# A two-layer decoder trunk in fp32 pairs: forget gates beside a values projection, shifted weight tiles, a second bank for retention, and another border between the layers

## Chip, cores and metric

The kernel runs on one core of a Trainium2 chip. The metric is the device time of one execution in microseconds; before the change the median of three runs was 1018.92 (1017.69 to 1019.12).

## What is computed

One sequence of 512 tokens of width 1024 passes two layers, each with a normalization ahead and a residual sum behind, and a last normalization. The core of the reference:

```python
def even_layer(x, g_norm, w_in, b_f, w_out):
    z = rms_norm(x, g_norm) @ w_in
    qa, ka, va, ga, fa, qb, kb, vb, gb = jnp.split(z, cuts, axis=-1)
    log_f = jax.nn.log_sigmoid(fa.astype(f32) + b_f.astype(f32))
    ya = forgetting_attention(hA(qa), hA(ka), hA(va), log_f).reshape(Bsz, S, WIDTH_FOX)
    yb = dilated_attention(hB(qb), hB(kb), hB(vb)).reshape(Bsz, S, WIDTH_DIL)
    y = jnp.concatenate([ya * jax.nn.silu(ga), yb * jax.nn.silu(gb)], axis=-1)
    return x + y @ w_out

def odd_layer(x, g_norm, w_in, w_out):
    z = rms_norm(x, g_norm) @ w_in
    q, k, v, g = jnp.split(z, [qk_w, 2 * qk_w, 2 * qk_w + v_w], axis=-1)
    q = rotate(q.reshape(Bsz, S, N_HEADS_RET, RET_QK_DIM))
    k = rotate(k.reshape(Bsz, S, N_HEADS_RET, RET_QK_DIM)) * (RET_QK_DIM ** -0.5)
    y = retention(q, k, v.reshape(Bsz, S, N_HEADS_RET, RET_V_DIM))
    y = head_group_norm(y).reshape(Bsz, S, v_w).astype(x.dtype)
    return x + (y * jax.nn.silu(g)) @ w_out
```

Layer 0 has 16 forgetting heads (causal softmax attention whose logits get differences of the running sum c of log_f, one gate for each of the 16 heads and each token) and 16 dilated heads, all 64 wide. Layer 1 has 4 retention heads with q and k 256 wide and v and gate 512 wide: o at token t is the sum over s up to t of a decay times (q_t . k_s) v_s, then a normalization over the head.

## The kernel before, in words

Tokens are held as 4 tiles of 128. `xres` is the residual stream (token on the partition), and `xT` is the normalized input, transposed (feature on the partition). Every factor of a wide matmul is kept as two fp32r numbers, a high part and the rest, and a product is three matmuls, hi·hi, hi·lo and lo·hi, by `three` (L199, L200, L201). `split` makes the pair: ScalarE copies the high part (L140), VectorE subtracts it (L142).

*Weights* come in chunks of 512 KB in the order of a list, `plan`. `load_next` issues the DMA of the next one from SP into one of three buffers `w_raw`; `split_next` splits the oldest into `w_h` and `w_l`, 1,024 floats per partition each, in two operations of 512 on each engine; `weights` hands out the oldest split chunk.

*Layer 0* has 8 head groups of 4 heads in the order D F F F F D D D (D dilated, F forgetting). A group's projections are its values by `proj_tokens` (result `pt`, token on the partition: the stationary operand is a block of xT, the moving one 256 columns of the weights; two chunks, 96 matmuls), its keys and queries by `proj_features` (result `pf`: weights stationary, 512 columns of xT moving; 48 × 2 matmuls), and its gates, again by `proj_features`. The attention of a head goes in steps of one query block: logits into `ps_s`, VectorE adds the bias and takes the smallest, ScalarE takes the exponential, POOL divides (`softmax_block`); a head later its blocks are transposed into `ps_pt` and split (`transpose_block`), then multiplied with the values into `ps_o` (`pv_block`); `finish_head` forms y, POOL multiplies it by the gate, and a split makes `yh` and `yl`. `interleave` spreads fillers over the steps of a group by their estimated time: the group's gate projection, the next group's values, an output projection where `OUTS` has one (result `po`, added to xres at L296), and the next group's keys and queries. In the last group, 7, the filler beside its gates is the output projection of groups 5 and 6.

*Forget gates* (`forget_gates`) run as the first filler of group 0: 16 matmuls with the 16 gate columns of the weights into `pfa` (L381, L382), the bias by ScalarE, four transposes into `ps_zt` (L387), the log sigmoid in some fifteen small operations on VectorE and ScalarE (tile `fg`), transposes into `ps_lt` (L425), a running sum by VectorE's scan (L430), transposes into `ps_ct` (L433), and a DMA to `c_dram`. `fox_bias` loads a head's row from there into all partitions (`cs`) and lets POOL make the bias of a block.

*The border*: after group 7 its output projection runs by token tile (`last_out`, two chunks, 12 matmuls per tile). After a tile's half, `last_tile` takes its sum of squares (L127) and POOL multiplies the half by the gain of layer 1 (L584); after both halves come the reciprocal root (`rstd_of`, L105 to L111), the scaling by ScalarE (L588), transposes into `ps_xt` (L151), and the split into xT.

*Layer 1*: head 0's projections come before any head's steps: values (`proj_tokens` twice), gate g by `proj_wide` (result `pw`, 512 columns of weights moving), keys and queries. `rotate_done` rotates k and q, with POOL and a split at the end. Then per head `scores` (`ps_a`), `retain` (the sums into the bank `ps_r`; statistics, `yn` at L773 by VectorE, the gate on POOL at L774), and `y_block` (transposes into `ps_yt`, L782), spread over fillers, which are the next head's projections and the previous one's output projection. Accumulators of TensorE: three banks for projections (pool `pp`), two for logits and scores (`ps_s`), two for transposes (`ps_t`) and one (`ps_o`) for a head's output and `ps_r`.

The order on POOL is as the program is written; on the other engines a scheduler of the framework sets it.

## Time and profile before

| | |
|---|---|
| three runs | 1019.12, 1017.69, 1018.92 us, median 1018.92 |
| the profiled execution | 1019.2 us, of which the span of the trace is 1017.2 |
| mean granted clock of TensorE | 0.996 of full |
| TensorE (PE) busy | 992.6 us, 98% of the span, 5,170 matmuls |
| weight loads (PEld) | 840.3 us, beside the matmuls |
| VectorE (DVE), ScalarE (ACT), POOL busy | 637.0, 481.6, 240.0 us |
| DMA | 100.5 MB, mean 99 GB/s |

A row of a timeline gives the start and the length of one instruction in microseconds, its engine, line, operation, "written tile<-tiles read", the stationary operand's shape (of a matmul) and the written one's, and in brackets how long the engine was idle before it and what released it. Matmuls overlap: one starts before the last has ended, so what each costs is the spacing from start to start. A row of the waits gives the waiting engine, tile and line, what it waited for, and the total in microseconds, the count and the longest one. A group's row gives the count, the busy time, the mean length in ns, and the idle time ahead with its releasers.

### The profile page before, as it was taken

Reading aid. Unit: us, or ns where it says so; the run is one execution under the profiler, and the core shown is the slowest. Engines: PE = TensorE matmul, PEld = TensorE weight load, DVE = VectorE, ACT = ScalarE, POOL = GpSimd, SP = SyncE. Lnnn points to the kernel's source line nnn. Section 1 sums busy time; section 2 is a strip of 40 time slices with the busy share of each in tenths; the row PEclk is TensorE's granted clock in tenths of the full one; section 3 lists DMA queues with packets and bytes.
Section 4 is the critical chain, followed back from the end, with each engine's and each line's share of the span. In section 5 each row is a group of like instructions: output and inputs, shape, how many; then the busy total and the mean of one; then the engine's idle time right before and its main releaser. Section 6 shows DMA issues by size and latency. Waiting matters only on the chain.

```text
span 1017.2 us, 14317 instructions
## 1 busy us (share of the span) xinstructions
PE 992.6 (98%) x5170; PEld 840.3 (83%) x5170; DVE 637.0 (63%) x1382; ACT 481.6 (47%) x987; POOL 240.0 (24%) x340
## 2 busy tenths in 40 slices
PE   8999999999999999999999989999999999999997
PEld 7878898898888988988988779877888888888875
DVE  6465676576576676665667773477545844683476
ACT  6355565555545645554657573333323332333233
POOL 1011444444344442211212130013100300030012
PEclk9999999999999999999999999999999999999999
DMA  7554677544557884337333125222222231322112
GB/s 205 115 127 87 137 91 98 146 100 93 140 101 111 120 91 128 81 66 136 72 110 99 58 65 189 83 84 83 83 63 84 84 102 62 104 84 83 63 42 83
DMA packets 73288, 100.50 MB, mean 99 GB/s; under 512 B 5233, under 2 KB 48497, under 8 KB 73090
## 3 DMA queue, kind: packets, MB, share of 16 engines
q1 hardware_dynamic: 73218, 99.60, 42.4%
q8 instruction: 40, 0.66, 0.3%
q14 instruction: 30, 0.25, 0.1%
HBM read 84.87 MB, written 2.13 MB: 86 GB/s over the span
## 4 chain that ended last, share of the span: by engine, by line
PE 86%; DVE 7%; ACT 2%; DMA 2%; issue 2%; POOL 1%; DVEq 0%; POOLq 0%; ACTq 0%; SPq 0%
PE pf L199 10%; PE pf L200 10%; PE pf L201 10%; PE pw L200 5%; PE pw L201 5%; PE pw L199 5%; PE po L199 5%; PE po L201 5%; PE po L200 5%; PE pt L201 3%; PE pt L199 3%; PE pt L200 3%; PE ps_pt L502 3%; PE ps_o L515 2%; PE ps_o L514 2%; PE ps_s L488 2%
## 5 line engine op out<-in xcount | busy, mean ns | idle before, releaser
L142 DVE TENSOR_TENSOR w_l<-w_raw,w_h 128x512 fp32r<-128x512 f32 x288 | 210.7, 758 | 97.7 <-ACT w_h L140 83.9
L140 ACT ACTIVATE w_h<-w_raw 128x512 fp32r<-128x512 f32 x288 | 169.8, 628 | 187.3 <-PE pf L200 56.3
L199 PE MATMUL pf<-xT,w_h 128*128 128x512 f32 x512 | 201.5, 394 | 0.0
L201 PE MATMUL pf<-xT,w_l 128*128 128x512 f32 x512 | 200.5, 392 | 0.0
L200 PE MATMUL pf<-xT,w_h 128*128 128x512 f32 x512 | 200.3, 391 | 0.0
L495 POOL TENSOR_SCALAR pi<-pi,st 128x512 f32<-128x512 f32 (+3 forms) x128 | 74.5, 583 | 363.4 <-DVE st L494 333.4
L201 PEld LDWEIGHTS pf<-xT,w_l 128*128 128x128 f32 x512 | 96.1, 188 | 21.1
L199 PEld LDWEIGHTS pf<-xT,w_h 128*128 128x128 f32 x512 | 96.2, 188 | 18.3
L200 PEld LDWEIGHTS pf<-xT,w_h 128*128 128x128 f32 x512 | 96.2, 188 | 18.1
L140 ACT ACTIVATE pth<-ps_pt 128x512 fp32r<-128x512 f32 (+3 forms) x128 | 55.2, 431 | 97.0 <-PE ps_pt L502 85.6
L201 PE MATMUL pt<-w_h,xT 128*128 128x256 f32 x320 | 90.8, 284 | 1.6 <-DVE xT L142 1.6
L199 PE MATMUL pt<-w_h,xT 128*128 128x256 f32 x320 | 91.4, 286 | 0.1
L200 PE MATMUL pt<-w_l,xT 128*128 128x256 f32 x320 | 90.8, 284 | 0.0
L199 PE MATMUL pw<-w_h,xT 128*128 128x512 f32 x224 | 88.4, 395 | 0.0
L200 PE MATMUL pw<-w_l,xT 128*128 128x512 f32 x224 | 87.9, 393 | 0.0
L201 PE MATMUL pw<-w_h,xT 128*128 128x512 f32 x224 | 87.9, 392 | 0.0
L493 ACT ACTIVATE pi<-pi,st 128x512 f32<-128x512 f32 (+3 forms) x128 | 71.5, 559 | 33.4 <-DVE st L491 32.7
L774 POOL TENSOR_TENSOR yn<-yn,gate 128x512 f32<-128x512 f32 x16 | 21.0, 1313 | 265.0 <-DVE yn L773 255.5
L296 DVE TENSOR_TENSOR xres<-po,xres 128x512 f32<-128x512 f32 x88 | 59.6, 684 | 26.4 <-PE po L201 26.0
L142 DVE TENSOR_TENSOR ptl<-ps_pt,pth 128x512 fp32r<-128x512 f32 (+3 forms) x128 | 62.3, 488 | 20.4 <-ACT pth L140 18.6
L201 PEld LDWEIGHTS pt<-w_h,xT 128*128 128x128 f32 x320 | 61.2, 191 | 1.8 <-DVE xT L142 1.8
L199 PEld LDWEIGHTS pt<-w_h,xT 128*128 128x128 f32 x320 | 61.1, 191 | 1.1 <-ACT xT L140 0.6
(178 smaller groups left out, 1898.0 us busy)
## 6 DMA issues: line engine op xcount, KB each, us to landing
w_raw<-in_even_w_in_dram SPq DMA_DIRECT2D x64, 512.0 KB, 5.4
w_raw<-in_odd_w_in_dram SPq DMA_DIRECT2D x48, 512.0 KB, 3.6
w_raw<-in_even_w_out_dram SPq DMA_DIRECT2D x16, 512.0 KB, 4.1
w_raw<-in_odd_w_out_dram SPq DMA_DIRECT2D x16, 512.0 KB, 3.5
qb<-qa SPq DMA_DIRECT2D x32, 128.0 KB, 2.8
qb<-qa SPq DMA_DIRECT2D x16, 256.0 KB, 3.2
qa<-qa SPq DMA_DIRECT2D x32, 128.0 KB, 3.0
cs<-c_dram SPq DMA_DIRECT2D x16, 256.0 KB, 3.6
```

What stands on the lines that cost most here:

```text
L140: act.activation(hi, src, AF.Copy, scale=scale)
L142: dve.tensor_tensor(lo, src, r32(hi), ALU.subtract)
L199: pe.matmul(ps, lhsT=ah, rhs=bh, start=first, stop=False)
L200: pe.matmul(ps, lhsT=ah, rhs=bl, start=False, stop=False)
L201: pe.matmul(ps, lhsT=al, rhs=bh, start=False, stop=last)
L296: dve.tensor_tensor(xr, ps, xr, ALU.add)
L488: pe.matmul(ps[:, 0:n], lhsT=q[:, 1, qs], rhs=k[:, 0:n], start=False, stop=True)
L493: act.activation(pi[:, 0:n], pi[:, 0:n], AF.Exp, bias=st[:, 0:1], scale=-1.0, accum_out=st[:, 1:2])
L495: pool.tensor_scalar(pi[:, 0:n], pi[:, 0:n], st[:, 2:3], 1.0, ALU.mult, ALU.mult)
L502: pe.transpose(pt[:, (i - j) * P:(i - j + 1) * P], hs["p"][i][:, j * P:(j + 1) * P], ident)
L514: pe.matmul(po[:, j * P:S], lhsT=v, rhs=th[:, 0:n], start=(j == 0), stop=False)
L774: pool.tensor_tensor(yn, yn, r["g"][:, i, :], ALU.mult)
```

## The change

1. The 16 gate columns ride in the values projection of the first forgetting group (`proj_more`, 96 matmuls with 272 columns in place of 256, result `pm`). The 16 matmuls into `pfa` and the transposes into `ps_zt` go. The gate chain is cut in three: `forget_gates` behind that projection, `forget_sums` at step 14 of the 16 of the next keys projection, `forget_turn` at step 5 of the queries. The gate weights and the bias come with the constants.
2. The chunks of all other token projections ("v") start 8 floats (32 bytes) into their tiles, which are 1,088 floats wide.
3. `retain` alternates between the `ps_o` bank and one of `ps_s`; head 0 of layer 1 projects keys and queries ahead of its gate.
4. Group 6's output projection leaves group 7's filler and joins group 7's in `last_out` (four chunks, 24 matmuls per token tile, some in tiles of q, y and v that are free by then). At the end of group 7 two chunks of layer 1 are split ahead.
5. The gain of layer 1 is folded into its weights: each 128-row block is split with a scale per partition (chunks 256 columns wide take four operations on each engine in place of two; those 512 wide take two, as before). POOL's multiplies and the load of the gain into all partitions go.

```diff
-OUTS = {1: (0,), 2: (1,), 3: (2,), 4: (3,), 5: (4,), 7: (5, 6)}
+OUTS = {1: (0,), 2: (1,), 3: (2,), 4: (3,), 5: (4,), 7: (5,)}
...
+            if tiles:
+                h, l = tiles(shape)
+            else:
+
+                n, at = (16, 0) if de == "f" else (0, 8 if de == "v" else 0)
+                h, l = (wp.tile([P, WCH], F32R, tag=tag, name=name)[:, at:at + 1024 + n * shape[1]].rearrange(
+                    "p (k c) -> p k c", k=shape[1]) for tag, name in (("wh", "w_h"), ("wl", "w_l")))
+            src, h_, l_ = raw, h, l
+            if de == "f":
+                fw = late["fw"].pop(0)
+                split(h[:, :, 256:], l[:, :, 256:], fw)
...
+            if kt0 is not None:
+                for k in range(shape[1]):
+                    split(h_[:, k], l_[:, k], src[:, k], scale=gain1[:, kt0 + k:kt0 + k + 1])
...
+    def proj_more(w, c0, done):
+
+        chunks = [(w[kc * 512:(kc + 1) * 512, c0:c0 + 256], "f", None, None) for kc in range(2)]
+
+        def work():
+            ws = [weights() for _ in range(2)]
+            for t in range(NT):
+                ps = pp.tile([P, S], F32, tag="p", name="pm")[:, 0:272]
+                ts_ = slice(t * P, (t + 1) * P)
+                for kt in range(KT):
+                    h, l = ws[kt // 4]
+                    three(ps, xT[:, 0, kt, ts_], xT[:, 1, kt, ts_], h[:, kt % 4, :], l[:, kt % 4, :],
+                          kt == 0, kt == KT - 1)
+                    if kt == KT - 1:
+                        done(t, ps)
+                    yield 1.6 * MM
+        return chunks, work(), 51 * MM
...
-        r["proj"] = v + g + qk if hd == 0 else qk + g + v
+        r["proj"] = v + qk + g if hd == 0 else qk + g + v
...
+            dma(out=bf, in_=even_b_f[0].partition_broadcast(P))
+            dma(out=fw, in_=win[:, 4096:4112].rearrange("(k p) c -> p k c", p=P))
+            dma(out=gain1, in_=odd_norm[0].rearrange("(k p) -> p k", p=P))
...
+        def forget_z(t, ps):
+
+            if t == 0:
+                fg["t"] = ap_.tile([P, 8, NT * 16], F32, tag="bias", name="fg", bufs=3)
+            dve.tensor_tensor(fg["t"][:, 0, t * 16:(t + 1) * 16], ps, bf, ALU.add)
...
-            raw = cst.tile([P, KT, 16], F32, name="fw")
-            dma(out=raw, in_=win[:, 4096:4112].rearrange("(k p) c -> p k c", p=P))
-            hl = cst.tile([P, KT, 32], F32R, name="fwhl")
-            split(hl[:, :, 0:16], hl[:, :, 16:32], raw)
-            pf = pp.tile([P, S], F32, tag="p", name="pfa")
-            for kt in range(KT):
-                pe.matmul(pf[0:32, :], lhsT=hl[:, kt, :], rhs=xT[:, 0, kt, :], start=kt == 0, stop=False)
-                pe.matmul(pf[0:16, :], lhsT=hl[:, kt, 0:16], rhs=xT[:, 1, kt, :], start=False, stop=kt == KT - 1)
-            z = ap_.tile([32, S], F32, tag="cs", name="fz", bufs=2)
-            act.activation(z, pf[0:32, :], AF.Identity, bias=bf, scale=1.0)
-            zt = ps_t.tile([P, NT, 32], F32, tag="t", name="ps_zt")
-            for t in range(NT):
-                pe.transpose(zt[:, t, :], z[:, t * P:(t + 1) * P], ident[0:32, 0:32])
...
+            dma(out=c_dram, in_=c_hs)
...
-            dma(out=c_dram, in_=c_hs)
...
+                forget_z(t, ps[:, 256:272])
+                if t == NT - 1:
+                    forget_gates()
...
-            hs = slice(c * H, (c + 1) * H)
-            pool.tensor_tensor(xn[:, hs], xres[:, t, hs], late["gain1"][:, hs], ALU.mult)
...
-                    act.activation(xn[:, hs], xn[:, hs], AF.Copy, scale=late["r"])
+                    act.activation(xn[:, hs], xres[:, t, hs], AF.Copy, scale=late["r"])
...
+        def in_v(shape):
+            hl = gp.tile([P, 2] + shape[1:], F32R, tag="v", name="w_hl")
+            return hl[:, 0], hl[:, 1]
...
+        def ahead(n):
+            for _ in range(n):
+                split_next()
+            yield 0.0
...
-        last_out = out_of(7, by_tile=last_tile)
+        last_out = out_of(6, 7, by_tile=last_tile, homes={1: in_q, 2: in_y, 3: in_v})
...
+                nxt = nxt[:1] + [at(nxt[1], {14: forget_sums}), at(nxt[2], {5: forget_turn})]
...
-            f += nxt[1:]
+            f += nxt[1:] if n < 7 else [([], ahead(2), 0.0)]
...
-            po = ps_o.tile([P, S], F32, tag="o", name="ps_r")
+
+            po = ps_s.tile([P, S], F32, tag="s", name="ps_r") if i % 2 else ps_o.tile([P, S], F32, tag="o", name="ps_r")
```

What this moves on TensorE, at three places. First the forget gates: before, the end of their matmuls, and behind it the start of group 0's gate projection (`pf_659`), with the transposes into `ps_zt` in it.

```order
L381 MATMUL pfa<-xT,fwhl 32x512
L382 MATMUL pfa<-xT,fwhl 16x512
L381 MATMUL pfa<-xT,fwhl 32x512
L382 MATMUL pfa<-xT,fwhl 16x512
L199 MATMUL pf_659<-xT,w_h 128x512
L200 MATMUL pf_659<-xT,w_h 128x512
L201 MATMUL pf_659<-xT,w_l 128x512
L199 MATMUL pf_659<-xT,w_h 128x512
L387 MATMUL ps_zt<-ident,fz 128x32 x4
L200 MATMUL pf_659<-xT,w_h 128x512
L201 MATMUL pf_659<-xT,w_l 128x512
```

After, these stand only as columns of `pm`; the transposes for the sums come late in the keys projection of the first forgetting group (`pf_924`).

```order
L212 MATMUL pf_924<-xT,w_h 128x512
L213 MATMUL pf_924<-xT,w_l 128x512
L211 MATMUL pf_924<-xT,w_h 128x512
L212 MATMUL pf_924<-xT,w_h 128x512
L213 MATMUL pf_924<-xT,w_l 128x512
L461 MATMUL ps_lt<-ident,fg 16x128 x4
L211 MATMUL pf_924<-xT,w_h 128x512
L212 MATMUL pf_924<-xT,w_h 128x512
```

What moved: `pfa` and `ps_zt` are gone from the start of group 0's stage, and `ps_lt`, which stood late in the gate projection of that group, stands 42 keys matmuls behind `pm`.

Second the border: before, `po` of the last group ends and the first values projection of layer 1 (`pt_6738`) begins, with the third token tile's transposes in it.

```order
L199 MATMUL po<-w_h,yh 128x512
L200 MATMUL po<-w_l,yh 128x512
L201 MATMUL po<-w_h,yl 128x512
L199 MATMUL pt_6738<-w_h,xT 128x256
L200 MATMUL pt_6738<-w_l,xT 128x256
L201 MATMUL pt_6738<-w_h,xT 128x256
L151 MATMUL ps_xt<-ident,xn 128x128 x4
L199 MATMUL pt_6738<-w_h,xT 128x256
L151 MATMUL ps_xt<-ident,xn 128x128 x4
```

After, the second tile's transposes stand among the last output matmuls of the third (`w_hl` is a chunk in a tile of v; the last row is the fourth tile's).

```order
L211 MATMUL po<-w_hl,yh 128x512
L212 MATMUL po<-w_hl,yh 128x512
L213 MATMUL po<-w_hl,yl 128x512
L211 MATMUL po<-w_hl,yh 128x512
L153 MATMUL ps_xt<-ident,xn 128x128 x4
L212 MATMUL po<-w_hl,yh 128x512
L153 MATMUL ps_xt<-ident,xn 128x128 x4
L213 MATMUL po<-w_hl,yl 128x512
L211 MATMUL po<-w_h,yh 128x512
```

What moved: 22 output matmuls of the next tile stand between a tile's last product and its transposes, and the values projection starts after the fourth tile's.

Third the first scores of layer 1 (`ps_a`): before, they stand among the keys projection of head 1 (`pf_7293`).

```order
L200 MATMUL pf_7293<-xT,w_h 128x512
L201 MATMUL pf_7293<-xT,w_l 128x512
L199 MATMUL ps_a<-qh,kh 128x512
L199 MATMUL pf_7293<-xT,w_h 128x512
L200 MATMUL pf_7293<-xT,w_h 128x512
L201 MATMUL pf_7293<-xT,w_l 128x512
L200 MATMUL ps_a<-ql,kh 128x512
L201 MATMUL ps_a<-qh,kl 128x512
L199 MATMUL ps_a<-qh,kh 128x512
```

After, they stand behind head 0's gate projection (`pw`), which fills the time from the queries' end.

```order
L211 MATMUL pw<-w_h,xT 128x512
L212 MATMUL pw<-w_l,xT 128x512
L213 MATMUL pw<-w_h,xT 128x512
L211 MATMUL ps_a<-qh,kh 128x512
L212 MATMUL ps_a<-ql,kh 128x512
L213 MATMUL ps_a<-qh,kl 128x512
L211 MATMUL ps_a<-qh,kh 128x512
L212 MATMUL ps_a<-ql,kh 128x512
L213 MATMUL ps_a<-qh,kl 128x512
L211 MATMUL pf_7319<-xT,w_h 128x512
```

What moved: 96 gate matmuls now lie between the end of the queries projection and the scores, where before the keys of head 1 were cut in between them. Further on, between the first and the second `ps_r`, stand 18 matmuls in place of 28, and between the first `ps_r` and the first `ps_yt` 42.

More of the change, by code (lines that the diff above doesn't have):

```diff
@@ L201, in three, with proj_features @@
         pe.matmul(ps, lhsT=al, rhs=bh, start=False, stop=last)
-    def proj_features(w, c0, done, deinterleave=False):
-        chunks = [(w[kc * 512:(kc + 1) * 512, c0:c0 + 256], deinterleave) for kc in range(2)]
+    def proj_features(w, c0, done, deinterleave=False, gain=False):
+        chunks = [(w[kc * 512:(kc + 1) * 512, c0:c0 + 256], deinterleave, None, 4 * kc if gain else None)
+                  for kc in range(2)]
         def work():
@@ L222, in proj_features, with proj_tokens @@
         return chunks, work(), 48 * MM
-    def proj_tokens(w, c0, done, by_tile=False):
-        chunks = [(w[kc * 512:(kc + 1) * 512, c0:c0 + 256], False) for kc in range(2)]
+    def proj_tokens(w, c0, done, by_tile=False, gain=False):
+        chunks = [(w[kc * 512:(kc + 1) * 512, c0:c0 + 256], "v", None, 4 * kc if gain else None)
+                  for kc in range(2)]
         def work():
@@ L246, in proj_tokens, with fourth @@
         return chunks, work(), 48 * MM
+    def fourth(shape):
+        return [late["wpool"].tile(shape, F32R, tag=f"w{n}", name=f"w_{n}") for n in "hl"]
+    def proj_more(w, c0, done):
[13 more added lines that the diff above has]
+        return chunks, work(), 51 * MM
     def proj_wide(w, c0, done):
-        chunks = [(w[kc * 256:(kc + 1) * 256, c0:c0 + 512], None if kc == 3 else False) for kc in range(4)]
+        chunks = [(w[kc * 256:(kc + 1) * 256, c0:c0 + 512], False, fourth if kc == 3 else None, 2 * kc)
+                  for kc in range(4)]
         def work():
@@ L273, in work, with out_proj @@
                             yield 3 * MM
[L274 removed]
+                    if o and (kc < 3 or (loaded and loaded[0][2])):
                         split_next()
         return chunks, work(), 96 * MM
[L278 removed]
+    def out_proj(y, w, rows, by_tile=None, homes={}):
         nc_, nk = len(rows), 2 * len(rows)
[L284 removed]
+        chunks = [(w[r:r + 256, cq * 512:(cq + 1) * 512], False, homes.get(nc_ * cq + i), None)
                   for cq in range(2) for i, r in enumerate(rows)]
@@ L422, in forget_gates, with forget_sums @@
             dve.scalar_tensor_tensor(lf, pol, -2.0, mz, ALU.mult, ALU.add)
+            fg["lf"] = lf
+        def forget_sums():
+            lf = fg["lf"]
+            c_hs = ap_.tile([16, S], F32, tag="bias", name="c_hs", bufs=3)
             lt = ps_t.tile([16, S], F32, tag="t", name="ps_lt")
```

95 lines of the change are left out of this document (51 added, 44 removed).

## Prediction

> **What bounds the kernel now.** First the page of the profile: the span, the engines' busy time, and the chain of work that ended last.
>
> ```profile
> span 1017.2 us, 14317 instructions
> ...
> PE 992.6 (98%) x5170; PEld 840.3 (83%) x5170; DVE 637.0 (63%) x1382; ACT 481.6 (47%) x987; POOL 240.0 (24%) x340
> ...
> PE 86%; DVE 7%; ACT 2%; DMA 2%; issue 2%; POOL 1%; DVEq 0%; POOLq 0%; ACTq 0%; SPq 0%
> ```
>
> TensorE is busy for 98% and carries 86% of the chain. Time can only go if matmuls go, if each takes less, or if the few waits go. So I read next the list of TensorE's waits, and of it the rows at the places that the change touches (forget gates, scores and retention of layer 1, the border between the layers).
>
> ```profile
> PE ps_r L199 <- DVE yn L773: 2.3, 1, 2.3
> PE ps_xt L151 <- ACT xn L588: 2.0, 2, 1.6
> ...
> PE pt L201 <- DVE xT L142: 1.6, 1, 1.6
> ...
> PE ps_a L199 <- ACT qh L140: 0.8, 1, 0.8
> PE ps_lt L425 <- DVE fg L422: 0.8, 1, 0.8
> PE po L199 <- DVE xres L296: 0.6, 1, 0.6
> PE po L199 <- ACT yh L140: 0.4, 1, 0.4
> PE ps_a L200 <- DVE ql L142: 0.4, 1, 0.4
> PE ps_ct L433 <- DVE c_hs L430: 0.4, 1, 0.4
> ```
>
> These are 9.3 us. Third, the engines' busy time in three stretches: the last head group, the border, and the first projection of layer 1 (columns: us; PE, PEld, DVE, ACT, POOL busy; granted clock; DMA share; GB/s).
>
> ```profile
> 534.00:580.00 46.00, 45.05 (x234) 36.63 (x233) 32.40 (x89) 28.55 (x67) 11.30 (x18) 1.00 0.24 78
> 580.00:612.00 32.00, 27.26 (x168) 22.91 (x167) 25.18 (x52) 22.44 (x48) 11.44 (x9) 1.00 0.25 77
> 612.00:633.00 21.00, 21.00 (x148) 19.75 (x148) 8.31 (x13) 7.34 (x13) 0.00 (x0) 1.00 0.62 209
> ```
>
> The border leaves TensorE idle for 4.7 us; in the other two it is nearly full.
>
> **The change, part by part.** The sum stands against the profiled execution, 1019.2 us (the span and 2.0 us around it); the median of the three runs, 1018.9, is 0.3 below it.
>
> The yardstick is the spacing of wide matmuls on the timeline, here eleven from start to start:
>
> ```profile
> 695.03 0.39 PE L200 MATMUL pf<-xT,w_h 128*128 128x512 f32 x1
> ...
> 697.52 0.39 PE L199 MATMUL pw<-w_h,xT 128*128 128x512 f32 x1
> ```
>
> 2.49 / 11 = 0.227 us for 512 columns. A matmul lasts 0.39 but the next starts after 0.227, so a wait that empties the array costs about 0.16 beyond the wait that is listed.
>
> *Forget gates.* The 16 matmuls into pfa and the transposes into ps_zt go:
>
> ```profile
> 51.35 0.40 PE L381 MATMUL pfa<-xT,fwhl 128*32 128x512 f32 x1
> ...
> 55.05 0.40 PE L199 MATMUL pf<-xT,w_h 128*128 128x512 f32 x1
> ...
> 55.75 0.40 PE L199 MATMUL pf<-xT,w_h 128*128 128x512 f32 x1
> 56.08 0.43 PE L387 MATMUL ps_zt<-ident,fz 32*128 32x32 f32 x4
> 56.44 0.51 PE L200 MATMUL pf<-xT,w_h 128*128 128x512 f32 x1
> ...
> 67.95 0.60 PE L425 MATMUL ps_lt<-ident,fg 128*16 128x128 f32 x4 [0.78 <-DVE fg L422]
> ```
>
> Matmuls: 55.05 − 51.35 = 3.7. Transposes: 56.44 − 55.75 − 0.23 = 0.5. The waits at ps_lt and ps_ct: 0.8 + 0.4 + 2 × 0.16 = 1.5. They go if the chain of gate operations is covered: in the new order the sums come 42 projection matmuls after the last gate column (9.5 us, and the attention steps between them some 4 more), and the chain took 11.5 us from the transposes, 56.44, to the end of the wait for it, 67.95. Added: 96 matmuls of 272 columns in place of 256, 1,536 columns, 0.7. **−5.0**; −3.5 if both waits stay. The c_dram store is issued later, behind five weight loads in SP's queue, and two loads of cs stand behind it; what waits for it is POOL's bias of the first forgetting head, whose probabilities are transposed only a head (four steps) later; those steps hide it, and I cost it at nothing. If that cover were gone, POOL's in-order queue would hold back the normalizations behind it, and TensorE behind those, by the length of one such wait, 0 to 2 us as the waits above go; the range has room for it.
>
> *The 32 bytes.* 864 of the 960 token-projection matmuls (ten projections of 96, without the joined one) get a moving operand that starts 32 bytes past a multiple of 64. Before, all operands start on one. What they take now (39 per line in the stretch), beside matmuls of the same width with other operands:
>
> ```profile
> L200 PE MATMUL pt<-w_l,xT x39: 283/283/283, 611.8 to 625.5; 128*128 128x256 f32 x39
> ```
> ```profile
> 681.78 0.28 PE L199 MATMUL ps_a<-qh,kh 128*128 128x256 f32 x1
> 681.89 0.28 PE L200 MATMUL ps_a<-ql,kh 128*128 128x256 f32 x1
> ```
>
> From 611.8 to 625.5 are 38 × 3 spacings: 13.7 / 114 = 0.120 us. Half of a wide matmul is 0.113; scores stand 0.11 apart. So 0.007 to 0.010 of each is something other than columns, and no wait shows there. No row has a shifted operand; the bounds are the 0.110 of the scores, 864 × 0.0102 = 8.8 us saved, zero, and above it the slowest pair of narrow matmuls with the clock at full:
>
> ```profile
> 203.49 0.31 PE L514 MATMUL ps_o<-pth,v 128*128 128x128 f32 x1
> 203.63 0.27 PE L515 MATMUL ps_o<-ptl,v 128*128 128x128 f32 x1
> ```
>
> 0.14, which would cost 864 × 0.020 = 17.3 us. That the two operands, the moving one and the stationary one being loaded for the next matmul, meet when both start on multiples of 64 bytes is a guess; it fits that the extra is there at 256 columns, where the next load (0.19 long in the records) outlasts the spacing, more than at 512. I take the column rate: 864 × (0.120 − 0.1132) = **−5.9**.
>
> The Trainium skill ("TensorE: Matmul & The Clock Gate", "LDWEIGHTS (loading the stationary operand)") gives 106.7 ns for loading 128 columns, and under "Back-to-back issue gap" N/2.4 + 2.5 ns between matmuls, 109 ns at 256. The 0.120 of the trace is above both, so neither names what takes the rest; if the shift brought the spacing to that rule, an estimate from the page is 864 × 0.011 = 9.5 us.
>
> *Weights scaled.* 20 of 48 chunks of layer 1 are split in four pieces of 256 instead of two of 512, on ScalarE and VectorE alike:
>
> ```profile
> L142 DVE TENSOR_TENSOR w_l<-w_raw,w_h 128x512 fp32r<-128x512 f32 x288 | 210.7, 758 | 97.7 <-ACT w_h L140 83.9
> ```
> ```profile
> L142 DVE TENSOR_TENSOR ptl<-ps_pt,pth 128x256 fp32r<-128x256 f32 x32 | 13.5, 422 | 1.0 <-ACT pth L140 0.8
> ```
>
> 4 × 0.42 − 2 × 0.76 = 0.2 us more per chunk, 20 × 0.2 = 4 us if it lay open. It lies beside matmuls: from 612 to 633 VectorE is busy 8.3 and ScalarE 7.3 of 21 us. Zero. The tiny loads that come in with the constants, and the 512 KB gain that no longer goes, are on SP away from the chain: zero.
>
> *The border.* POOL's multiplies go:
>
> ```profile
> L584 POOL TENSOR_TENSOR xn<-xres,gain 128x512 f32<-128x512 f32 x8 | 10.2, 1292 | 7.2 <-DVE rs L107 3.1 <-DVE xres L296 2.7 <-DVE var L129 0.7
> ```
>
> The border's five waits are 2.0 + 1.6 + 0.6 + 0.4 = 4.6, with 5 × 0.16 = 5.4. Two ways through it, on TensorE's timeline, are from the last head's last product to the wait for its yh, and from the last output matmul to the last tile's transposes:
>
> ```profile
> 580.17 0.28 PE L515 MATMUL ps_o<-ptl,v 128*128 128x128 f32 x1
> ...
> 585.14 0.50 PE L199 MATMUL po<-w_h,yh 128*128 128x512 f32 x1 [0.40 <-ACT yh L140]
> ...
> 596.67 0.40 PE L201 MATMUL po<-w_h,yl 128*128 128x512 f32 x1
> ...
> 603.08 0.65 PE L151 MATMUL ps_xt<-ident,xn 128*128 128x128 f32 x4 [0.48 <-ACT xn L588]
> ```
>
> The second took 603.08 − 596.67 − 0.40 = 6.0; without the multiply of 1.29 it is 4.7. Now 24 output matmuls stand per token tile instead of 12, 22 of them (5.0 us) between a tile's end and its transposes: covered, but for the first tile, which loads a table on top; 0 to 1 us is left there, I take 0.2. The first took 5.0, part of it in queues that the smaller border load shortens; 9 matmuls (2.1 us) now cover it, so 1 to 2.9 is left, I take 1.4. With two drains 1.9 stays. 5.4 − 1.9: **−3.5** (−5.4 to −1).
>
> *The last head group pays for it.* 48 output matmuls (10.9 us) leave its filler: 45.1 − 10.9 = 34.2 us of TensorE work. VectorE's 32.4 loses two chunks' splits (4 × 0.76) and gains the two split ahead (8 × 0.42): 32.7, or 95% of that. ScalarE has 28.6. The matmuls aren't lost, they run in the border; but where VectorE's chain becomes longer than TensorE's work, waits appear. Between nothing and the whole 10.9 I take **+2**, near nothing, since what TensorE idles there now is only 0.95 of 46 with VectorE at 70%, and the two splits ahead are waited for by nobody before the border's end.
>
> *Scores and retention of head 0.* With the gates' projection behind q's, 96 matmuls stand between q's rotation and the first scores: 0.8 + 0.4 + 2 × 0.16 = 1.5 goes. The second retention has its own bank, so it no longer waits for yn: 2.3 + 0.16 = 2.5 goes. Behind that wait came slow matmuls:
>
> ```profile
> 691.17 0.39 PE L201 MATMUL ps_r<-vh,al 128*128 128x512 f32 x1
> ...
> 701.47 0.49 PE L201 MATMUL ps_r<-vh,al 128*128 128x512 f32 x1
> ...
> 705.11 0.27 PE L782 MATMUL ps_yt<-ident,yn 128*128 128x128 f32 x1
> ```
>
> Nine in 3.64 us, 0.40 each: 3.64 − 9 × 0.227 = 1.6 goes too. What is late next is the transpose of yn, which needs POOL:
>
> ```profile
> 700.27 1.29 POOL L774 TENSOR_TENSOR yn<-yn,gate 128x512 f32<-128x512 f32 x1 [11.01 <-DVE yn L773]
> ```
>
> From 691.17 to 701.56 are 10.4 us; the new order puts 42 matmuls there, 9.5. With the drain 1.0 is left. 1.5 + 2.5 + 1.6 − 1.0: **−4.6** (−6 to −3). The Trainium skill ("TensorE: Matmul & The Clock Gate", "Part 1: The HAM clock gate") has the clock halve after an idle window of about 3.4 us; here a wait of 2.3 was enough. By that rule the slow stretch is no sure part of the wait, and the sum would be 1.6 us less.
>
> Sum: −5.0 − 5.9 − 3.5 + 2 − 4.6 = −17.0. 1019.2 − 17.0 = 1002.2, as a median 0.3 less: **1001.9 us**.
>
> **The rivals.**
> (a) The shift reaches the floor of the scores, −8.8 in place of −5.9: 999.0. For it: the same width runs at 0.11. Against it: there the loads have other operands. The 109 ns of the Trainium skill (same page and section as above) would be this case, with −9.5 at 998.3.
> (b) The shift does nothing: 1001.9 + 5.9 = 1007.8. For it: nothing in the trace says that addresses matter; the extra may come from loading a new stationary operand every 0.12 us.
> (c) The last head group becomes VectorE's: its stretch keeps 46 us though its filler shrank, +10.9 in place of +2: 1010.8. For it: 95%. Against it: the steps of a head lie four apart, so that VectorE's and TensorE's work overlap.
> (d) Slower: the shifted operand costs. It decides from where a shifted matmul takes 864 × d = 11.1, the rest of the sum, d = 0.013, so a spacing of 0.133; at 0.14 it is 1001.9 + 5.9 + 17.3 = 1025.1. Against it: the shift adds no column and no byte, and no row shows a price for an address, since all are alike.
>
> **How the numbers follow.** Forecast 0.45 (its own range 997 to 1006), (a) 0.08, (b) 0.25, (c) 0.13, (d) 0.07, and 0.02 that losses elsewhere eat the gain. About 0.2% (2 us) is what a measurement here tells from none. All but the last two are faster: 0.91; same 0.02; slower 0.07. The range takes the forecast, (a), (b) and (c): 995 to 1011; (d) and (c) with (b) together (1017) are left out.
>
> **What would show it.** In the profile after: TensorE's idle time (span less busy, 24.6 us now) down by some 8; rows of pt with 0.113 spacing outside the joined projection (0.120 means (b), over 0.13 (d)); no pfa, no waits at ps_lt, ps_ct, ps_r and ps_a; at most two at the border; the last group's stretch near 35 us and not 46. I am wrong if the last group is the longer, if pt got slower, or if the first forgetting head waits for its bias.

## The result and the profile after

| | before | after |
|---|---|---|
| median | 1018.31 us (1016.51 to 1019.12, 4 runs) | 1007.91 us (1006.93 to 1008.66, 4 runs) |
| span of the profiled execution | 1017.2 us | 1006.0 us |

The ratio is 0.990, with a 95% interval of 0.988 to 0.992. The kernel became 10.4 us faster, where 17 were forecast: the time lies inside the whole range (995 to 1011), outside the forecast's own (997 to 1006), and almost on what was written for the rival in which the shift does nothing (1007.8). That is not what happened, as the runs below show. The intervals of the runs reach some 1.5 us to either side, so what is said below of terms near 1 us rests on the traces more than on the medians.

The same three rows of the page after the change:

```profile
span 1006.0 us, 14334 instructions
...
PE 984.2 (98%) x5150; PEld 834.5 (83%) x5150; DVE 644.5 (64%) x1427; ACT 496.9 (49%) x1029; POOL 230.9 (23%) x331
...
PE 85%; DVE 5%; ACT 3%; issue 2%; DMA 2%; POOL 2%; SPq 0%; DVEq 0%; POOLq 0%; ACTq 0%
```

TensorE is idle for 21.8 us in place of 24.6: only 2.8 us of the 11.2 came from there, where some 8 were forecast. Most of the rest is busy time: fewer columns (3.0), narrow matmuls that stand closer (2.2) and slow ones that went (1.6). Of its waits, the rows that are new or that answer to the old ones:

```profile
PE pt L211 <- ACT w_h L142: 1.5, 2, 0.8
PE ps_yt L851 <- POOL yn L843: 1.3, 1, 1.3
...
PE pw L212 <- DVE w_l L146: 1.2, 1, 1.2
PE ps_o L565 <- DVE y L580: 1.1, 2, 0.7
...
PE po L211 <- ACT yh L142: 0.7, 1, 0.7
PE po L213 <- DVE y1l L144: 0.7, 1, 0.7
...
PE ps_s L539 <- DMA qa<-qa: 0.3, 1, 0.3
```

All of ps_lt, ps_ct, ps_r and ps_a are gone, as forecast; pw, y1l and two at y and qa have come. The first row, at pt, lies in the first 17 us, where the kernel before had other waits: its first keys projection began at 29.56 us, this one's at 29.39. The engines' busy time in the last head group, the border, and the rest of the border with layer 1's first values (columns as before the change: us; PE, PEld, DVE, ACT, POOL busy; granted clock; DMA share; GB/s):

```profile
529.00:566.00 37.00, 35.33 (x190) 28.27 (x190) 32.32 (x92) 29.27 (x70) 12.12 (x18) 1.00 0.26 83
566.00:592.00 26.00, 25.21 (x117) 19.87 (x116) 16.77 (x44) 18.03 (x40) 1.29 (x1) 1.00 0.20 61
592.00:605.00 13.00, 12.90 (x109) 12.63 (x110) 5.04 (x12) 6.23 (x13) 0.00 (x0) 1.00 0.57 201
```

The last head group shrank from 46 to 37 us with VectorE at 87%; the border's idle time went from 4.7 to 0.9 (566 to 605 us).

For a ledger I took every spacing of TensorE from start to start, subtracted the columns' time (0.2264 us for 512), and summed what is over 0.15 us in each stretch. The columns themselves fell by 3.0 us (3.6 for the gate matmuls, less 0.7 for the added columns).

| term | forecast | found | from |
|---|---|---|---|
| forget gates | −5.0 | −3.5 | run without it |
| the shift | −5.9 | −2.2 | run without it |
| border and last group | −1.5 | −3.2 | stretch: 7.6 to 4.4 us of excess |
| scores and retention, head 0 | −4.6 | −4.0 | stretch: 5.4 to 1.4 us |
| wait at the gate's weights (pw) | 0 | +1.6 | stretch: 0 to 1.6 us |
| wait at y1l near the end | 0 | +0.7 | stretch: 0.8 to 1.5 us |
| sum | −17.0 | −10.6 | the medians differ by 10.4, the spans by 11.2 |

### The profile page after: what moved, and what is told of

It reads as the page before. It is cut to its first block, busy times and chain, and to the rows that moved or that the text cites. A ratio compares the mean times of both kernels' runs of the same rounds, so it can differ in the third digit from the quotient of the medians.

```text
span 1006.0 us, 14334 instructions
## 1 busy us (share of the span) xinstructions
PE 984.2 (98%) x5150; PEld 834.5 (83%) x5150; DVE 644.5 (64%) x1427; ACT 496.9 (49%) x1029; POOL 230.9 (23%) x331
## 4 chain that ended last, share of the span: by engine, by line
PE 85%; DVE 5%; ACT 3%; issue 2%; DMA 2%; POOL 2%; SPq 0%; DVEq 0%; POOLq 0%; ACTq 0%
PE pf L211 10%; PE pf L212 10%; PE pf L213 10%; PE po L213 6%; PE po L211 5%; PE po L212 5%; PE pw L212 5%; PE pw L213 5%; PE pw L211 5%; PE pt L211 3%; PE pt L213 3%; PE ps_pt L553 3%; PE pt L212 3%; PE ps_o L566 2%; PE ps_s L539 2%
## 5 line engine op out<-in xcount | busy, mean ns | idle before, releaser
L144 DVE TENSOR_TENSOR w_l<-w_raw,w_h 128x512 fp32r<-128x512 f32 x190 | 138.7, 756 | 52.9 <-ACT w_h L142 41.2
L142 ACT ACTIVATE w_h<-w_raw 128x512 fp32r<-128x512 f32 x190 | 111.9, 624 | 90.9 <-PE pf L212 40.4
L146 DVE SCALAR_TENSOR_TENSOR w_l<-w_raw,small,w_h 128x256 fp32r<-128x256 f32 (+1 forms) x136 | 86.2, 669 | 33.1 <-ACT w_h L142 32.9
L142 ACT ACTIVATE w_h<-w_raw,small 128x256 fp32r<-128x256 f32 (+1 forms) x136 | 73.0, 596 | 66.5 <-PE pw L213 24.4
L211 PE MATMUL pt<-w_h,xT 128*128 128x256 f32 x288 | 81.5, 283 | 1.5 <-ACT w_h L142 1.5
L212 PE MATMUL pt<-w_l,xT 128*128 128x256 f32 x288 | 80.8, 280 | 0.0
L213 PE MATMUL pt<-w_h,xT 128*128 128x256 f32 x288 | 80.5, 280 | 0.0
L843 POOL TENSOR_TENSOR yn<-yn,gate 128x512 f32<-128x512 f32 x16 | 21.8, 1364 | 248.4 <-DVE yn L842 178.8
```

What stands on the lines that cost most here:

```text
L142: act.activation(hi, src, AF.Copy, scale=scale)
L144: dve.tensor_tensor(lo, src, r32(hi), ALU.subtract)
L146: dve.scalar_tensor_tensor(lo, src, scale, r32(hi), ALU.mult, ALU.subtract)
L211: pe.matmul(ps, lhsT=ah, rhs=bh, start=first, stop=False)
L212: pe.matmul(ps, lhsT=ah, rhs=bl, start=False, stop=False)
L213: pe.matmul(ps, lhsT=al, rhs=bh, start=False, stop=last)
```

## The experiments

### What the shift is

Five kernels differ from the changed one only in where the operands of the token projections start. The first has no shift:

```diff
-                n, at = (16, 0) if de == "f" else (0, 8 if de == "v" else 0)
+                n, at = (16, 0) if de == "f" else (0, 0)
```

> The changed kernel with the values' weights back at the start of their tiles (multiples of 64 bytes); everything else as changed. Theory 1 (the trace after the change: pt spacing 0.1172 in place of 0.1197 us): the shift is worth 864 x 0.0025 = 2.2 us, so about 1010.1 us, and the spacing of pt is 0.1197 again. Theory 2 (the step on record: the shift is worth 5.9 us and something else took it back): about 1013.8 us. Theory 3 (the shift is worth nothing and the spacing fell for another reason): 1007.9 us, spacing still 0.117.

It took 1010.09 us (1009.91 to 1010.30; ratio to before 0.9918, 0.9904 to 0.9931), 2.2 more than the changed kernel. Theory 1 holds in time and in spacing. In the others `at` is 16 (64 bytes) and 32 (128 bytes), or the transposed input is moved:

```diff
-    xT = keep.tile([P, 2, KT, S], F32R, name="xT")
+    xT = keep.tile([P, 2 * KT * S + 16], F32R, name="xT")[:, 8:8 + 2 * KT * S].rearrange(
+        "p (h k s) -> p h k s", h=2, k=KT)
```

(with 32 in place of 16 in the last one, where the tiles behind it move by 128 bytes and not 64).

> The changed kernel with the values' weights 64 bytes into their tiles in place of 32. If what counts is the start modulo 64 bytes, this is no shift at all: pt spacing 0.1197 us, the time that of the kernel without a shift (1010 us by theory 1). If any start off the tile's own start helps (another region, another tile), spacing 0.117 and 1007.9 us.

> The changed kernel with the values' weights 128 bytes into their tiles. In the runs so far pt took 0.1197 us with the moving operand's start at 0 and the stationary one's at 0 modulo 128, and 0.117 with a distance of 32 or 64. Theory 1 (the distance of the two starts modulo 128 bytes counts, zero is the dear case): 0.1197, 1010.1 us, as without a shift. Theory 2 (any shift off a multiple of 256 bytes helps): 0.117, 1007.9 us.

> The changed kernel with the transposed input moved by 32 bytes too, so that in token projections both operands start 32 bytes past a multiple of 64, and in feature projections the moving one alone does. If the distance of moving and stationary operand modulo 64 counts (the guess on record that the two meet), pt goes back to 0.1197 us and loses 2.2 us; if the moving operand's own start counts, pt stays at 0.117. The feature projections (1536 matmuls of 512 columns at 0.227 to 0.231 us) gain at most 0.002 each, 3 us, if their moving operand's start counts as well, nothing if they run at their columns' rate already: 1005 to 1010 us.

> The changed kernel with the transposed input at 32 bytes past a multiple of 256 and the values' weights at 160, so that the moving and the stationary operand of pt start at a distance of 128 bytes, both 32 past a multiple of 64. Theory 1 (their distance modulo 128 counts): pt at 0.1197 us. Theory 2 (the moving operand's own start off a multiple of 64 counts): pt at 0.117. By both, pf and pw pay for the moved input as in the run with both shifted (pf 0.233 in place of 0.229, pw 0.233 in place of 0.227 us), some 11 us over 1536 and 672 matmuls: 1020 us by theory 1, 1018 us by theory 2.

One row for each, all for the hi·lo matmuls of layer 1's second values projection (the last 33 of them; the spacing is the distance from the first to the last start, over 96). The changed kernel:

```profile
L212 PE MATMUL pt<-w_l,xT x33: 277/280/281, 605.2 to 616.4; 128*128 128x256 f32 x33
```

Without a shift:

```profile
L212 PE MATMUL pt<-w_l,xT x33: 283/283/283, 606.7 to 618.3; 128*128 128x256 f32 x33
```

64 bytes:

```profile
L212 PE MATMUL pt<-w_l,xT x33: 280/280/280, 605.0 to 616.3; 128*128 128x256 f32 x33
```

128 bytes:

```profile
L212 PE MATMUL pt<-w_l,xT x33: 279/281/285, 607.2 to 618.6; 128*128 128x256 f32 x33
```

Both operands 32 past a multiple of 64, at a distance of 64:

```profile
L213 PE MATMUL pt<-w_l,xT x33: 279/279/279, 609.8 to 621.1; 128*128 128x256 f32 x33
```

Both 32 past, at a distance of 128:

```profile
L213 PE MATMUL pt<-w_l,xT x33: 279/281/285, 610.5 to 621.9; 128*128 128x256 f32 x33
```

| moving start less stationary start, modulo 256 bytes | spacing over this projection | time of the kernel |
|---|---|---|
| 0 | 0.120 us | 1010.09 |
| 32 | 0.117 | 1007.91 |
| 64 | 0.118 | 1008.12 (1007.55 to 1008.21) |
| 64, both 32 past a multiple of 64 | 0.118 | 1017.81 (1016.49 to 1018.59) |
| 128 | 0.119 | 1010.42 (1009.41 to 1011.59) |
| 128, both 32 past | 0.119 | 1019.65 (1019.13 to 1021.93) |

A shift by 64 bytes does the same as one by 32, so the start modulo 64 is not what counts. What the six runs agree on is the distance of the two starts: dear at 0, best at 32 and 64, between them at 128. My theory "modulo 128" had 128 as dear as 0, and that is nearly so: the single matmuls scatter there from 279 to 285 ns, and about a third of the gain is left in this projection. But over the 526 spacings of layer 0 (from 60 to 580 us) that follow one another directly the averages are 0.1197 us without a shift, 0.1194 and 0.1189 at 128, and 0.1171 to 0.1174 at 32 and 64, and the kernel's time at 128 shows no gain. In no run did the average come to the columns' 0.113.

The moving operand's own start is not excluded by the table: moving the input also moved the weights' tiles behind it, so in the order of the rows that start lies 0, 32, 64, 96, 128 and 160 bytes past a multiple of 256, and it orders the six as well. The joined projection (`pm`) speaks for the distance. The blocks of its weights start 1,088 bytes apart, so 0, 64, 128 and 192 past a multiple of 256. With the input unmoved (nine kernels) the spacings behind them average 0.1265, 0.1254, 0.1268 and 0.1253 us. In the two kernels with a moved input a block whose own start is at 0 stands at a distance of 224, and takes 0.1248 and 0.1254, not 0.1265. These are differences of 1 to 2 ns, so the distance is likely and not shown.

The two kernels with a moved input are 10 us slower for another reason, told in advance for the first of them only as a gain of up to 3 us: wide matmuls pay for it. Gate projections (`pw`, 512 columns, stationary operand now 32 past a multiple of 64), eleven spacings of the kernel with both moved, and eleven of the changed kernel:

```profile
655.07 0.40 PE L212 MATMUL pw<-w_h,xT 128*128 128x512 f32 x1
...
657.64 0.39 PE L214 MATMUL pw<-w_h,xT 128*128 128x512 f32 x1
```
```profile
641.55 0.39 PE L211 MATMUL pw<-w_h,xT 128*128 128x512 f32 x1
...
644.04 0.39 PE L213 MATMUL pw<-w_h,xT 128*128 128x512 f32 x1
```

2.57 / 11 = 0.234 us against 2.49 / 11 = 0.226. The feature projections, whose moving operand is the moved input, went from 0.229 to 0.233 on average. With 1,536 of these, at 0.004 more, and 672 of `pw`, at 0.006 more on average, that makes the 10 us. So a 512-column matmul takes 0.004 to 0.007 us more when one operand, whichever, starts 32 bytes past a multiple of 64. In no run do both operands of such a matmul start there, so their distance may be what counts in this too.

### The forget gates

The old functions and the filler were put back into the changed kernel, in two versions that differ in a pad ahead of the constants:

```diff
+                f.append(([], gates(), 6.0))
-                nxt = nxt[:1] + [at(nxt[1], {14: forget_sums}), at(nxt[2], {5: forget_turn})]
...
-            with_f = kind == "F" and j == 0
+            with_f = False
...
-        cst.tile([P, 48], F32, name="pad_cst")
+        cst.tile([P, 56], F32, name="pad_cst")
```

(the pad in the second version only).

> The changed kernel with the old forget gates: 16 matmuls of their own, two sets of transposes more, the chain at the start of group 0; all values projections 256 wide with the shift. Theory 1 (the traces: 2.9 us of matmul time saved, the waits of 1.5 us replaced by others of the same size in the keys and queries behind): the joined gates are worth 3 us, so 1011 us here. Theory 2 (the step on record, 5.0 us): 1012.9 us.

> The run with the old forget gates again, with a pad of 56 in place of 48 floats ahead of its constants, so that no stationary operand starts 32 bytes past a multiple of 64 (in the first one those of half of layer 0's output matmuls, of the probabilities' transposes and of the logits did, through the smaller bias tile). Theory 1 (those starts cost about 1.5 us, the joined gates are worth 3 to 4.5 us): 1011 to 1012.4 us, and po at 0.2284 us in place of 0.2299. Theory 2 (the starts cost nothing, the joined gates are worth 5.7 us): 1013.6 us.

The first took 1013.58 us (1012.79 to 1015.38), which spoke for the step on record; but in it the stationary operands of half the output matmuls, among others, stood 32 bytes past a multiple of 64. With the pad it was 1011.41 us (1010.27 to 1012.09; ratio to before 0.9934, 0.9921 to 0.9947). The joined gates are worth 3.5 us, and the misplaced starts had cost 2.2 (1.7 by the spans of the two profiles). The waits from 50 us until the first forgetting group's stage, first with the old gates (padded), then in the changed kernel:

```profile
PE ps_lt L465 <- DVE fg L462: 0.7, 1, 0.7
PE ps_ct L473 <- DVE c_hs L470: 0.4, 1, 0.4
```
```profile
PE ps_o L565 <- DVE y L580: 0.7, 1, 0.7
PE ps_s L539 <- DMA qa<-qa: 0.3, 1, 0.3
```

What the change took from the two gate waits came back behind VectorE and a DMA, in the same size. The wait for y, 0.7, is in every run with the new chain but the next one; the one for the DMA is anything from 0 to 1.4. I tried to take the first of these away by moving the sums behind the keys' evacuations:

```diff
-                nxt = nxt[:1] + [at(nxt[1], {14: forget_sums}), at(nxt[2], {5: forget_turn})]
+                nxt = nxt[:1] + [nxt[1], at(nxt[2], {1: forget_sums, 5: forget_turn})]
```

> The changed kernel with the sums of the forget gates at step 1 of the queries in place of step 14 of the keys. Theory 1 (the new wait of 0.97 us at ps_o for y, in the queries, comes from VectorE's queue, in which the copy and the scan, 1.9 us, stand among the keys' evacuations): that wait goes or shrinks, 1007 us. Rival (the chain is then late: waits at ps_ct, or POOL's bias late for the first forgetting head): 1008 to 1010 us, with a wait at ps_ct or at ps_pt for POOL early in the next group.

It took 1012.05 us (1011.17 to 1013.73): the rival. The waits of the same stretch:

```profile
PE ps_pt L553 <- POOL pi L546: 2.6, 1, 2.6
PE ps_ct L474 <- DVE c_hs L466: 2.3, 1, 2.3
PE ps_o L565 <- DVE y L580: 0.2, 1, 0.2
```

The wait at y did shrink, from 0.7 to 0.2. But the sums are late for their transposes by 2.3 us, and POOL, which must make the bias of the first forgetting head from them, waits for their way through `c_dram`:

```profile
111.21 0.69 POOL L595 TENSOR_SCALAR bias<-cs,c_th 128x512 f32<-128x512 f32 x1 [5.73 <-DMA cs<-c_dram]
```

Behind that wait of 5.7 us it holds up the probabilities by 2.6. In the changed kernel the load landed at 101.28 us and POOL began this bias at 104.12, without a wait. So the cover that the prediction relied on, when it costed this wait at nothing, is there: about 2.8 us.

### The order and the bank in layer 1

The old order of head 0's projections:

```diff
-        r["proj"] = v + qk + g if hd == 0 else qk + g + v
+        r["proj"] = v + g + qk if hd == 0 else qk + g + v
```

> The changed kernel with head 0's projections of layer 1 in the old order: values, gate, keys and queries. Theory 1 (the trace after the change: the waits of 1.5 us at the first scores went, but a wait of 1.3 and slow matmuls, 1.7 us in all, came at the gate's projection, whose weights' low part stands behind ql on VectorE): the order is worth nothing, 1007.9 us within 0.7, with waits at ps_a and none at pw. Theory 2 (the step on record: the order is worth 1.5 us): 1009.4 us.

It took 1008.95 us (1008.14 to 1010.97), between the two theories. The trace decides only for layer 1. Waits of this kernel, from the list:

```profile
PE ps_s L538 <- DMA qa<-qa: 1.2, 1, 1.2
...
PE ps_a L212 <- DVE ql L144: 0.7, 1, 0.7
PE ps_a L211 <- ACT qh L142: 0.6, 1, 0.6
```

The scores' waits return, 1.6 us with the drains (the 0.16 or so that an emptied array costs on top of each), and none at pw is left; in the changed kernel the excess at pw is 1.6. So the order gave back in layer 1 what it took. The profile of this run is 1.4 us longer for two things in layer 0, where the two programs are alike: its first keys projection begins at 30.41 us in place of 29.39, and the wait for a DMA at ps_s is 1.2 in place of 0.3 (in other runs with this layer 0 it was 0, 0.8 and 1.4). Whether they also explain the median I can't say.

Where the wait at pw comes from, VectorE's, POOL's and TensorE's timelines of the changed kernel:

```profile
641.77 1.47 DVE L146 SCALAR_TENSOR_TENSOR w_l<-w_raw,small,w_h 128x512 fp32r<-128x512 f32 x1
643.39 2.39 DVE L144 TENSOR_TENSOR ql<-rt,qh 128x512 fp32r<-128x512 f32 x2
645.70 0.75 DVE L146 SCALAR_TENSOR_TENSOR w_l<-w_raw,small,w_h 128x512 fp32r<-128x512 f32 x1
```
```profile
641.40 1.29 POOL L786 TENSOR_TENSOR rt<-rt,rt 128x512 f32<-128x512 f32 x1 [9.82 <-DVE rt L784]
642.65 1.74 POOL L787 TENSOR_TENSOR rt<-rt,rt 128x512 f32<-128x512 f32 x1
```
```profile
644.95 0.39 PE L211 MATMUL pw<-w_h,xT 128*128 128x512 f32 x1
646.50 0.50 PE L212 MATMUL pw<-w_l,xT 128*128 128x512 f32 x1 [1.17 <-DVE w_l L146]
```

The low part of the gate's weights (645.70) stands behind ql, whose second half waits for the rotation on POOL to end. And the two operations of VectorE that run while POOL rotates, the split at 641.77 and the first half of ql, take 1.5 us each; the second half of ql, in the same row, takes 0.69, and the split behind it 0.75. With the old order the weights had no rotation ahead of them.

One bank for all retentions:

```diff
-            po = ps_s.tile([P, S], F32, tag="s", name="ps_r") if i % 2 else ps_o.tile([P, S], F32, tag="o", name="ps_r")
+            po = ps_o.tile([P, S], F32, tag="o", name="ps_r")
```

> The changed kernel with all retentions in the one bank ps_o again, head 0's projections staying in the new order. Theory 1 (the step on record: the wait for yn of 2.3 + 0.16 and the slow matmuls behind it, 1.6, return, and the wait of 1.4 at the transposes of yn goes): 1007.9 + 2.7, 1010.6 us, with a wait at ps_r of over 2 us. Rival (the new order alone took the wait, as the steps stand later): 1008 us and no wait at ps_r.

It took 1010.12 us (1009.37 to 1011.43; ratio to before 0.9922, 0.9907 to 0.9937), 2.2 more than with two, and its span is 2.9 longer: theory 1. TensorE's timeline there, with the wait and two of the slow matmuls behind it:

```profile
691.17 0.50 PE L211 MATMUL ps_r<-vh,ah 128*128 128x512 f32 x1 [2.36 <-DVE yn L842]
...
693.25 0.63 PE L213 MATMUL pw<-w_h,xT 128*128 128x512 f32 x1
693.67 0.63 PE L211 MATMUL pw<-w_h,xT 128*128 128x512 f32 x1
```

Spacing 0.42 us, as before the change; in the changed kernel, whose wait in this stretch is the one at ps_yt, 1.27 us, none is slow. That wait is cover that is short, as the last run shows, which moves nine matmuls ahead of the transposes:

```diff
-            interleave(steps_of(R[n], SCORES + REST), fill, UPTO)
+            interleave(steps_of(R[n], SCORES + REST), fill, UPTO if n else UPTO[:5] + (.40,) + UPTO[6:])
```

> The changed kernel with nine more of the next head's projection matmuls (2.0 us) ahead of the first transposes of yn in head 0 of layer 1, taken from the stretch behind them (the share of the fillers at the second retention 0.40 in place of 0.36). Theory 1 (the 1.4 us left at ps_yt is cover that is short by that much): the wait goes, nothing else is late, 1006.5 us. Rival (the wait only moves on, to the third retention or the second transposes): 1007.9 us, with a wait of over 1 us at ps_r or ps_yt.

It took 1006.93 us (1006.57 to 1008.38; ratio to before 0.9877, 0.9861 to 0.9894), the fastest of all, though its interval overlaps that of the changed kernel. The transposes of yn don't wait any more, and no other wait came in that stretch:

```profile
695.61 0.60 PE L851 MATMUL ps_yt<-ident,yn 128*128 128x128 f32 x4
```

### The border

The old border with the gain still folded into the weights:

```diff
-OUTS = {1: (0,), 2: (1,), 3: (2,), 4: (3,), 5: (4,), 7: (5,)}
+OUTS = {1: (0,), 2: (1,), 3: (2,), 4: (3,), 5: (4,), 7: (5, 6)}
...
-        last_out = out_of(6, 7, by_tile=last_tile, homes={1: in_q, 2: in_y, 3: in_v})
+        last_out = out_of(7, by_tile=last_tile)
...
-            f += nxt[1:] if n < 7 else [([], ahead(2), 0.0)]
+            f += nxt[1:]
```

> The changed kernel with the old border: group 6's output projection is again a filler of group 7, the last projection has one group, and no two chunks are split ahead; the gain stays folded into the weights. Theory 1 (excess of TensorE over its columns' time from the start of group 7 to the end of layer 1's first values: 16.2 us before, 12.0 after, of which 0.6 is the shift): the two-group border and the missing multiplies together give 3.6 us; if most of it is the cover of 24 matmuls, this run is 2 to 3.5 us slower than the changed kernel, 1010 to 1011.5 us, with waits at po, ps_xt and pt between the last head and layer 1. Rival (the missing multiplies of POOL and the shorter chain do it alone, the second group nothing): 1008 us and no wait of over 0.5 us there.

It took 1009.63 us (1009.47 to 1011.27; ratio to before 0.9917, 0.9903 to 0.9930), 1.7 more than the changed kernel. Its waits between the last head and layer 1:

```profile
PE pt L213 <- DVE xT L144: 0.9, 1, 0.9
PE po L211 <- DVE xres L333: 0.5, 1, 0.5
PE po L211 <- ACT yh L142: 0.4, 1, 0.4
PE ps_xt L153 <- DVE xT L144: 0.2, 1, 0.2
```

Both theories hold half of it. From the last group's start to the end of the border the excess is 7.6 us before, 5.3 here, and 4.4 in the changed kernel. So 2.3 us went with the folded gain alone (both waits at ps_xt for xn are gone, and pt's fell from 1.6 to 0.9), and the second group, with the two chunks split ahead, took 0.9 more by the trace and 1.7 by the medians: 1.9 saved in the border, 1.0 paid in the last group, where TensorE now idles for 1.7 us of 37.

## Why the prediction was right, and where it was not

The direction and the places were right: the waits that were to go went, and the range held the time. That it did is owed in part to the rivals that the range took in: the forecast's own, 997 to 1006, ended 2 us short. The 6 us between 1001.9 and 1007.9 come from these steps.

*The shift* ("I take the column rate", −5.9) was the step that was mis-sized: it measured −2.2. I took the spacing of a pair of score matmuls, 0.11, as a floor; that was one pair, the first behind a 512-column matmul. The rows around it, before the change:

```profile
681.55 0.39 PE L201 MATMUL pf<-xT,w_l 128*128 128x512 f32 x1
681.78 0.28 PE L199 MATMUL ps_a<-qh,kh 128*128 128x256 f32 x1
681.89 0.28 PE L200 MATMUL ps_a<-ql,kh 128*128 128x256 f32 x1
682.01 0.28 PE L201 MATMUL ps_a<-qh,kl 128*128 128x256 f32 x1
```

The spacing behind the second score matmul is 0.12 already. The twenty score spacings at 256 columns that follow one another directly average 0.1186, hardly better than pt's 0.120: 0.113 or 0.114 for the four first ones, 0.119 or 0.120 for the rest. In layer 0 it is the same: of 21 score pairs of this width behind a feature projection 20 stand 0.113 or 0.114 apart, the seven behind pt 0.118 or 0.120. So the column rate is what a narrow matmul showed behind a wide one; no stream of narrow ones reached it on average, and it was no value to take for one. The guess at the mechanism fell as well: multiples of 64 are not what meets. The rival that the shift does nothing gave the right time for the wrong reason: the shift gave 2.2, and the other terms together fell short of theirs by 2.7.

The 109 ns that the prediction sets beside this step are, in the Trainium skill ("TensorE: Matmul & The Clock Gate", "Back-to-back issue gap"), the gap of an isolated matmul; a stream of loads and matmuls is set by both there, so the figure does not say what this stream could reach. The least average here was 0.117.

*The forget gates* (−5.0) measured −3.5. The columns and transposes were right; the step that failed is "they go if the chain is covered". The chain was covered, and its operations then stood in VectorE's queue among the keys' evacuations, so that y was late there. A wait was removed and its cause, work on VectorE, was only moved. The bias that I had costed at nothing did cost nothing, with about 2.8 us to spare.

*Scores and retention* (−4.6) came to −4.0, with 1.4 left at the transposes of yn in place of 1.0. The 1.6 of slow matmuls in it are those of the profiled execution. That most executions had such a stretch shows in their mean granted clock, 0.994 to 0.997 in 14 of 15 executions of one series before the change, 0.998 or 0.999 in the four of the changed kernel; where it lay in them is not shown. But the step "Zero" for the weights' splits failed: not for the four operations in place of two, but because the new order put the rotation of q ahead of the gate's weights in VectorE's queue. I had named what is queued behind each new wait on SP and POOL and not on VectorE. It cost 1.6.

*The border and the last group* (−3.5 and +2) came to −3.2 together. The last group did not become VectorE's, at 87% of busy time: its excess grew by 1.0. The border kept one wait, at yh (0.7 and a drain), where I had 1.9 left.

*Near the end* a wait of 0.7 at y1l came; it is in the runs with two banks and not in the one with one, so it goes with the second bank, and I had not looked there.

## What to carry to other kernels

A wait that goes because its chain got cover leaves the chain's operations in some queue: look at which other operations stand behind them there, on every engine, before taking the whole wait as gained. Take as attainable the rate that a stream of such rows shows, not that of one pair behind other work. And when a small tile is moved or resized, look at where the operands behind it start: this kernel lost about 2 us to starts that nobody chose.

## What the runs showed of the hardware

Three things that I had not expected. The spacing of 256-column fp32r matmuls with a new stationary operand each changes with where the two operands start in SBUF, most likely with the distance of the starts: 0.120 us at a multiple of 256 bytes, 0.119 at 128, and 0.117 to 0.118 at 32 or 64. Why is not shown. Directly behind a 512-column matmul the first spacing was 0.113 or 0.114 without any shift. And 512-column matmuls took 0.004 to 0.007 us more when one operand started 32 bytes past a multiple of 64. A shift by 64 bytes gave about the time of one by 32, 1008.12 us against 1007.91, and leaves every start on a multiple of 64.

Slow matmuls, 0.43 us apart at 512 columns, stood in stretches of 3.4 us in which the granted clock was 0.50. Three of them, before the change, with the later sums and with more cover (columns as in the stretches above):

```profile
701.60:705.00 3.40, 3.40 (x10) 2.59 (x9) 2.96 (x10) 0.20 (x1) 0.00 (x0) 0.50 0.21 38
```
```profile
116.00:119.40 3.40, 3.40 (x9) 2.62 (x9) 1.90 (x3) 1.34 (x3) 0.00 (x0) 0.50 0.52 122
```
```profile
18.50:21.90 3.40, 3.40 (x17) 3.40 (x18) 3.01 (x7) 1.93 (x5) 1.23 (x5) 0.50 0.88 118
```

They came behind waits of 2.3 us before the change, 2.4 with one bank and 2.6 at ps_pt with the later sums, but not behind the 2.3 at ps_ct in that last run. With more cover the stretch came at the start of the kernel, behind two waits of 0.8 and 0.7 us with one matmul between them; its first keys projection began 1.7 us later than in the changed kernel for it. So the length of one wait does not decide alone. The Trainium skill ("TensorE: Matmul & The Clock Gate", "Part 1: The HAM clock gate") puts the halving after an idle window of about 3.4 us. The length of the slow stretches here agrees with such a window, the idle time ahead of them does not: no wait that they followed was longer than 2.6 us, and one of 2.3 was followed by none.
